# Buffer places: bias columns on the right side, pads, weights first

## The chip, the cores and the metric

The kernel runs on one core of one Trainium2 chip. The metric is the time of one execution in microseconds of the device, the median of several runs. The core has TensorE (PE; its weight loads are shown apart as PEld), VectorE (DVE), ScalarE (ACT), GpSimd (POOL) and SyncE (SP), which only issues DMAs here. They share the on-chip memory SBUF, in which an address counts the bytes along one of 128 partitions. Matmul results go to PSUM.

## The reference

One layer of a decoder trunk, x of 2048 x 1024 in float32. An RMSNorm, a projection to 4096 columns, then two branches: a diagonal complex state-space layer (S5) with a GLU, and a causal pooling mixer; both gated and merged, projected and added to x, and a last RMSNorm:

```python
h = _rmsnorm(x, norm_g[l])
proj = h @ w_in[l] + b_in[l]
ua, za, ub, zb, ga, gb = jnp.split(proj, SPLITS, axis=-1)
ya = _s5_branch(ua, ..., ssm_w_glu[l], ssm_b_glu[l])
ya = ya * jax.nn.silu(za)
yb = _pool_branch(ub, pool_w[l], pool_scale[l]) * jax.nn.silu(zb)
merged = (jax.nn.sigmoid(ga) * (ya @ w_branch_a[l])
          + jax.nn.sigmoid(gb) * (yb @ w_branch_b[l]))
x = x + merged @ w_out[l]
...
return _rmsnorm(x, final_norm_g)
```

`_s5_branch` ends in `y * sigmoid(y @ w_glu + b_glu)`.

## The kernel before, in words

Each large product is made of three matmuls in type float32r: weights and moving operand are split into a high and a low part, and `mm3` (L101 to L104) issues high x high (L102), high x low (L103) and low x high (L104). One matmul has 128x128 weights and up to 512 moving columns of 4 bytes, 2048 bytes in a partition. The 2048 positions are worked in four chunks c of 512.

The stages in order of time:
1. Norm, transposes and the first projection block (UA), into hT, the moving operand: four tiles of 32 KB a partition, high and low parts. Weights of the first two tiles lie in the rotating pool w (`wt`, two buffers), those of UA tiles 2 and 3 in `w_first2` and `w_first3` of pool d1 (L189), for all four chunks.
2. ZA projection with the scan's matrices in the background (pool d2): `matrices` (L424) loads C (`cn`) and B (`B1`, `B2`, L431, L432) by SP, and fp32 matmuls (`psk`) and transposes follow.
3. Pooling branch (UB, ZB; pool d3): the pooled tile is split into `plhl` and multiplied by `pw` into `psp`.
4. Gates GA and GB, with the scan in the background (pool d4; matmuls of 256 columns, `psx` and `psy`).
5. GLU (pools d5 and e5): weights `wg`, moving operand `yhl`, in two buffers.
6. Per chunk the branch products (weights `wt`, moving `yab`, outputs scaled by the gates `gt`), the merge into `mt`, and the output projection with `mt` as weights and `wo` as moving operand; the last piece has 256 columns. Then the final norm; its gains are the tile `gb` (L1141).

The order of the instructions is the order of the code; each engine takes its own in turn. Weights reach the matmuls through a queue of jobs: SP loads `raw` (two buffers), ScalarE makes the high part (L94), VectorE or GpSimd the low part (L96, L98), and `pump` issues one such step at fixed places.

A pool lies on the left or on the right side of SBUF. Left pools stack upwards from address 16512 (16384 bytes and four 32-byte constants lie below), right ones downwards from 229344, and a tile takes a multiple of 32 bytes. A pool that is closed gives its room to the next; an instruction that first touches such room waits for the last users of what lay there. So places set waits too. Pools in order: const, raw, w, stg (left), hT0 to hT2 (right), xp (right), par, d1 (left), and then those of the stages. const holds the bias columns `cols` and `half` (192 bytes each), `sgn` (8), `rcnt` (64), `RD` (64) and `PH` (128).

Of the kernel before, what the change touches and what calls it, by code (L numbers as in the profile page):

```python
# [9 lines left out]
F32 = mybir.dt.float32  # L10
F32R = mybir.dt.float32r
# [25 lines left out]
def hybrid_kernel(ctx: ExitStack, tc: tile.TileContext, x, norm_g, w_in, b_in, log_dt, lam_re, lam_im,  # L37
# [7 lines left out]
    outr = out[0].rearrange("(k j) d -> j k d", j=T)  # L45

    const = ctx.enter_context(tc.tile_pool(name="const", bufs=1))
    rawp = ctx.enter_context(tc.tile_pool(name="raw", bufs=2))
    wp = ctx.enter_context(tc.tile_pool(name="w", bufs=2))
    stg = ctx.enter_context(tc.tile_pool(name="stg", bufs=3))  # L50
# [4 lines left out]
    def sub(stack, name, side="left"):  # L55
        return stack.enter_context(tc.tile_pool(name=name, bufs=1, side=side, reuse_waits="tile"))
# [15 lines left out]
        return pms.tile([128, 512], F32, tag="ms", name=name)  # L72


    cols = const.tile([128, 48], F32, name="cols")
    half = const.tile([128, 48], F32, name="half")
    sgn = const.tile([128, 2], F32, name="sgn")
    rcnt = const.tile([128, 16], F32, name="rcnt")
    RD = const.tile([128, G // 2], F32, name="RD")
    PH = const.tile([128, 2, G // 2], F32, name="PH")  # L80

    def bcol(n):
        return cols[:, n:n + 1]
# [42 lines left out]
    hl = {}  # L126
# [58 lines left out]
    idn = par.tile([128, 128], F32, name="idn")  # L185
    s_d = ExitStack()
    d1 = sub(s_d, "d1")

    def w_first(key):  # L189
        t = d1.tile([128, 2, 1024], F32R, name=f"w_first{key[1]}")  # L190
        hl[key] = t
        return t[:, 0, :], t[:, 1, :], lambda r: r

    UA, ZA, UB, ZB, GA, GB = 0, 4, 8, 12, 16, 24
# [4 lines left out]
    for n in range(NB):  # L199
        w_in_job(n, plain if n < 2 else w_first)  # L200
# [10 lines left out]
    def ts(o, i, s1, o0, s2=None, o1=None):  # L211
        if s2 is None:
            V.tensor_scalar(out=o, in0=i, scalar1=s1, scalar2=None, op0=o0)
        else:
            V.tensor_scalar(out=o, in0=i, scalar1=s1, scalar2=s2, op0=o0, op1=o1)
# [6 lines left out]
    def pieces(v, bits, count):  # L222

        import struct
        if (v, bits, count) not in kept:
            res, left = [], v
            for _ in range(count - 1):
                m, e = math.frexp(left)
                q = math.ldexp(math.floor(m * 2 ** bits), e - bits)
                res.append(q)  # L230
                left -= q
            res.append(struct.unpack("f", struct.pack("f", left))[0])
            kept[v, bits, count] = res
        return kept[v, bits, count]
# [67 lines left out]
    def params(d, V, ldt, lam, dn):  # L302
# [61 lines left out]
        for h in range(2):  # L364
            r = slice(h * 64, (h + 1) * 64)
            V.tensor_copy(out=PH[r, 0], in_=ang[r, h::2])
        a0, a1, pn = PH[:, 0], PH[:, 1], d.tile([128, H], F32, name="pn")
        turn = pieces(64 * math.pi, 11, 4)
# [290 lines left out]
    def scan(d):  # L659
# [53 lines left out]
        def phases():  # L713
# [4 lines left out]
            for j in range(LV):  # L718
                ts(th[:, j], PH[:, 1], float(T << j), ALU.mult)
                ts(lo[:, j], PH[:, 0], float(T << j), ALU.mult)  # L720
            ts(n, th, 2.0 / math.pi, ALU.mult, MAGIC, ALU.add)
# [174 lines left out]
    for i in reversed(range(NB)):  # L896
# [23 lines left out]
        for k in range(2):  # L920
            n = min(T, win - 1 - k * T)
# [145 lines left out]
    for c in range(NCH):  # L1067
        t = yhl[c]
# [23 lines left out]
    d6 = sub(s_d, "d6")  # L1092
# [4 lines left out]
    def load_gate(c, n):  # L1097
        t = d6.tile([128, 2, 512], F32, tag="gt", bufs=3, name="gt")
        SP.dma_start(out=t, in_=Gd[n][c].rearrange("b p k -> p b k"))
        gts[c, n] = t  # L1100
# [22 lines left out]
    def finish(tt):  # L1123
# [12 lines left out]
            A.dma_start(out=outr[tt // 2, k0:k0 + 128, cs], in_=r[:, cs])  # L1136
        x2.pop(tt)

    load_gate(0, 0)
    load_gate(0, 1)  # L1140
    gb = d6.tile([128, D], F32, name="gb")  # L1141
# [82 lines left out]
```

## Time and profile before

| | us |
|---|---|
| median of 3 runs | 1236.32 (1235.59 to 1238.8) |
| the profiled execution | 1238.27 |
| its span, first to last instruction | 1236.4 |
| mean granted TensorE clock in it | 0.993 |

In the rows, L102 is a line of the code above, and `mm<-hT,wt` says that the instruction writes tile mm and reads hT and wt (numbers of buffers are left out). Matmuls are pipelined, so a row's duration says little of how fast they follow each other; the distance between the starts of two does. In the order of time, two neighbouring rows stand apart by that distance, to 0.01 us; over a run of many the mean is better. A bracket at a row's end is the idle time of the engine before it, and what ended it.

### The profile page before, as it was taken

What the parts mean: (1) busy time and instruction counts of PE and PEld (TensorE: products, weight loads), DVE (VectorE), ACT (ScalarE), POOL (GpSimd) and SP (SyncE); (2) the same over time, 40 slices, a digit from 0 to 9 for tenths busy, and PEclk for the clock granted to TensorE, in tenths of its full rate; (3) what the DMA queues carried; (4) which work ended last, traced back from release to release, by engine and by line L of the source; (5) the groups of instructions that cost most, each with busy time, mean ns of one, the idle gap of its engine ahead of it and who ended that gap; (6) DMA issues with size and microseconds to landing.
All of it is one profiled execution on the core that took longest, in us unless ns stands there. A gap on an engine that the chain in (4) does not pass through costs nothing. (4 is left out here: it accounts for less than half of the span.)

```text
span 1236.4 us, 14778 instructions
## 1 busy us (share of the span) xinstructions
PE 1205.5 (97%) x5413; PEld 975.1 (79%) x5413; DVE 730.8 (59%) x1310; ACT 395.3 (32%) x622; POOL 346.4 (28%) x232
## 2 busy tenths in 40 slices
PE   6999989999999999999999999999999999999996
PEld 5887867788888888888888888887878888888885
DVE  5586378153543668777788773046565855755615
ACT  6542211222222232443333432244333322322202
POOL 3321167011110212332334321234562312213312
PEclk9999989999999999999999999999999999999998
DMA  8413233201111232433334332178766553563502
GB/s 295 133 43 84 58 112 126 80 17 54 43 45 43 83 110 88 129 91 110 113 94 128 96 102 78 66 227 253 247 218 209 182 188 131 175 207 105 188 1 102
DMA packets 149783, 149.94 MB, mean 121 GB/s; under 512 B 23584, under 2 KB 111184, under 8 KB 149712
## 3 DMA queue, kind: packets, MB, share of 16 engines
q1 hardware_dynamic: 127424, 112.28, 30.6%
q10 hardware_dynamic: 22288, 36.73, 7.9%
q8 instruction: 42, 0.69, 0.2%
q14 instruction: 29, 0.24, 0.1%
HBM read 99.43 MB, written 49.55 MB: 120 GB/s over the span
## 5 line engine op out<-in xcount | busy, mean ns | idle before, releaser
L102 PE MATMUL mm<-hT,wt 128*128 128x512 f32 x960 | 382.5, 398 | 0.0
L103 PE MATMUL mm<-hT,wt 128*128 128x512 f32 x960 | 380.6, 396 | 0.0
L104 PE MATMUL mm<-hT,wt 128*128 128x512 f32 x960 | 379.9, 396 | 0.0
L104 PEld LDWEIGHTS mm<-hT,wt 128*128 128x128 f32 x960 | 180.8, 188 | 44.1
L103 PEld LDWEIGHTS mm<-hT,wt 128*128 128x128 f32 x960 | 181.1, 189 | 43.5 <-DVE hT L98 0.9
L102 PEld LDWEIGHTS mm<-hT,wt 128*128 128x128 f32 x960 | 181.2, 189 | 42.7
L96 POOL TENSOR_TENSOR wt<-raw,wt 128x1024 fp32r<-128x1024 f32 x30 | 85.5, 2849 | 316.5 <-ACT wt L94 316.5
L1027 ACT ACTIVATE go<-mm,half 128x512 f32<-128x512 f32 x64 | 43.9, 686 | 204.9 <-PE mm L104 190.2
L102 PE MATMUL mm<-yab,wt 128*128 128x512 f32 x256 | 101.2, 395 | 1.8 <-DVE gt L1160 1.8
L104 PE MATMUL mm<-yab,wt 128*128 128x512 f32 x256 | 101.0, 395 | 0.0
L103 PE MATMUL mm<-yab,wt 128*128 128x512 f32 x256 | 101.0, 395 | 0.0
L94 ACT ACTIVATE wt<-raw 128x1024 fp32r<-128x1024 f32 x62 | 65.5, 1057 | 60.7 <-PE mm L104 34.2
L1162 POOL TENSOR_TENSOR m<-gt 128x512 f32<-128x512 f32 x32 | 52.1, 1630 | 100.4 <-DVE gt L1160 71.6
L1121 POOL TENSOR_TENSOR r<-r,gb 128x512 f32<-128x512 f32 (+1 forms) x33 | 41.1, 1260 | 138.4 <-ACT xt L1118 138.3
L96 DVE TENSOR_TENSOR wt<-raw,wt 128x1024 fp32r<-128x1024 f32 x32 | 58.6, 1831 | 19.7 <-ACT wt L94 19.6
L845 ACT ACTIVATE st<-mm,half 128x512 f32<-128x512 f32 x32 | 22.1, 690 | 145.9 <-PE mm L104 114.5
L1160 DVE SCALAR_TENSOR_TENSOR gt<-gt,mm 128x512 f32<-128x512 f32 x64 | 42.3, 680 | 32.8 <-PE mm L104 27.9
L102 PEld LDWEIGHTS mm<-yab,wt 128*128 128x128 f32 x256 | 48.0, 187 | 14.4 <-issue 2.6
L104 PEld LDWEIGHTS mm<-yab,wt 128*128 128x128 f32 x256 | 48.0, 187 | 11.7
L103 PEld LDWEIGHTS mm<-yab,wt 128*128 128x128 f32 x256 | 48.0, 187 | 11.6
L104 PE MATMUL mm<-wo,mt 128*128 128x512 f32 (+1 forms) x136 | 52.0, 383 | 0.0
L103 PE MATMUL mm<-wo,mt 128*128 128x512 f32 (+1 forms) x136 | 52.0, 382 | 0.0
(272 smaller groups left out, 1920.3 us busy)
## 6 DMA issues: line engine op xcount, KB each, us to landing
xt<-in_x SPq DMA_DIRECT2D x32, 512.0 KB, 5.4
raw<-in_w_in SPq DMA_DIRECT2D x32, 512.0 KB, 4.4
Gd<-go ACTq DMA_DIRECT2D x64, 256.0 KB, 2.4
gt<-Gd SPq DMA_DIRECT2D x32, 512.0 KB, 4.8
raw<-in_w_branch_a SPq DMA_DIRECT2D x32, 256.0 KB, 3.1
raw<-in_w_branch_b SPq DMA_DIRECT2D x32, 256.0 KB, 3.5
out<-r ACTq DMA_DIRECT2D x32, 256.0 KB, 2.3
Ud<-uo ACTq DMA_DIRECT2D x16, 256.0 KB, 2.1
```

What stands on the lines that cost most here:

```text
L94: A.activation(hi, src, AF.Copy, scale=1.0 if scale is None else scale)
L96: (eng or V).tensor_tensor(out=lo, in0=src, in1=hi.bitcast(F32), op=ALU.subtract)
L102: PE.matmul(ps, lhsT=sh, rhs=mh, start=first, stop=False)
L103: PE.matmul(ps, lhsT=sh, rhs=ml, start=False, stop=False)
L104: PE.matmul(ps, lhsT=sl, rhs=mh, start=False, stop=last)
L845: A.activation(t, ps, AF.Tanh, bias=hcol(n), scale=0.5)
L1027: A.activation(o, ps, AF.Tanh, bias=hcol(n), scale=0.5)
L1121: GP.tensor_tensor(out=r, in0=r, in1=gb[:, cs], op=ALU.mult)
L1160: V.scalar_tensor_tensor(out=gt[:, b], in0=gt[:, b], scalar=1.0, in1=pss[b], op0=ALU.add, op1=ALU.mult)
L1162: GP.tensor_tensor(out=m, in0=gt[:, 0], in1=gt[:, 1], op=ALU.add)
```

## The change

It adds no instruction and moves none: on each engine the same instructions stand in the same order. It makes a second pool for constants, `constr`, on the right side, with the bias columns in it; puts an unused tile `lpad` of 192 bytes at the end of const and one of 128 bytes, `pad6`, at the start of d6; and allocates the two w_first tiles as soon as d1 is opened, ahead of its other tiles, and not when they are first used.

```diff
+    constr = ctx.enter_context(tc.tile_pool(name="constr", bufs=1, side="right"))
...
-    cols = const.tile([128, 48], F32, name="cols")
-    half = const.tile([128, 48], F32, name="half")
-    sgn = const.tile([128, 2], F32, name="sgn")
-    rcnt = const.tile([128, 16], F32, name="rcnt")
+    cols = constr.tile([128, 48], F32, name="cols")
+    half = constr.tile([128, 48], F32, name="half")
+    sgn = constr.tile([128, 2], F32, name="sgn")
+    rcnt = constr.tile([128, 16], F32, name="rcnt")
     RD = const.tile([128, G // 2], F32, name="RD")
     PH = const.tile([128, 2, G // 2], F32, name="PH")
+    const.tile([128, 48], F32, name="lpad")
...
     d1 = sub(s_d, "d1")
+    firsts = {n: d1.tile([128, 2, 1024], F32R, name=f"w_first{n}") for n in (2, 3)}
     def w_first(key):
-        t = d1.tile([128, 2, 1024], F32R, name=f"w_first{key[1]}")
-        hl[key] = t
+        t = hl[key] = firsts[key[1]]
...
+    d6.tile([128, 32], F32, name="pad6")
     load_gate(0, 0)
```

const shrinks from 672 bytes to 384, so the left pools behind it move down by 288; constr takes 480 bytes, so the right pools move down by 480. What remains of the address after the last multiple of 512 bytes, as the program allocates it:

| tile | role in matmuls | before | after |
|---|---|---|---|
| hT0 to hT3, yab, wo | moving, 512 columns (wo also 256) | 480 | 0 |
| yhl (two buffers) | moving, 512 | 288 | 0 |
| plhl | moving, 512 | 384 | 96 |
| uu, spl | moving, 256 | 288 | 0 |
| wt, wg, bt, mz, ca (scan) | weights | 288 | 0 |
| mt | weights | 160 | 0 |
| w_first2, w_first3 | weights | 192, 256 | 64, 64 |
| pw | weights | 384 | 96 |
| idn | moving in transposes | 288 | 0 |

Slices of these tiles start at multiples of 512 bytes further on (idn's one slice at its start), so they keep the remainder.

The other effect is on waits. On SP, at the start of stage 2, where the scan's matrices load (DMAHW and a number are the queues' own semaphores, PE_49 and Pool_49 those of engines), before:

```order
28 L427 DMA cn<-in_ssm_c_re 128x4x64 [waits DMAHW1_49,PE_49]
29 L427 DMA cn<-in_ssm_c_im 128x4x64 [waits DMAHW3_49]
30 L427 DMA cn<-in_ssm_c_re 128x4x64 [waits DMAHW4_49]
31 L431 DMA B_1320<-in_ssm_b_re 64x32x16 [waits DMAHW5_49]
32 L432 DMA B_1320<-in_ssm_b_im 64x32x16 [waits DMAHW6_49]
35 L478 DMA CAd_145<-ca 512x1x128 [waits DMAHW5_49,Pool_49]
```

The same place after:

```order
28 L429 DMA cn<-in_ssm_c_re 128x4x64 [waits DMAHW1_49,PE_49]
29 L429 DMA cn<-in_ssm_c_im 128x4x64 [waits DMAHW3_49]
30 L429 DMA cn<-in_ssm_c_re 128x4x64 [waits DMAHW4_49]
31 L433 DMA B_1324<-in_ssm_b_re 64x32x16 [waits DMAHW5_49,PE_49]
32 L434 DMA B_1324<-in_ssm_b_im 64x32x16 [waits DMAHW6_49]
35 L480 DMA CAd_148<-ca 512x1x128 [waits DMAHW5_49,Pool_49]
```

The first load of B1 gains a wait for a matmul: the last that reads w_first3. The first load of cn waits for the last that reads w_first2, and waited for an earlier one. On SP at the start of stage 6, before:

```order
356 L958 DMA raw<-in_w_out 128x1024 [waits DMAHW3_49,Pool_49]
357 L1099 DMA gt<-Gd_0_105 128x2x512 [waits DMAHW5_49,PE_49]
358 L1099 DMA gt<-Gd_0_109 128x2x512 [waits DMAHW0_49]
359 L1142 DMA gb<-in_final_norm_g 128x1024 [waits DMAHW1_49]
360 L1099 DMA gt<-Gd_0_113 128x2x512 [waits DMAHW2_49]
```

And after:

```order
356 L960 DMA raw<-in_w_out 128x1024 [waits DMAHW3_49,Pool_49]
357 L1101 DMA gt<-Gd_0_108 128x2x512 [waits DMAHW5_49,PE_49]
358 L1101 DMA gt<-Gd_0_112 128x2x512 [waits DMAHW0_49]
359 L1145 DMA gb<-in_final_norm_g 128x1024 [waits DMAHW1_49,PE_49]
360 L1101 DMA gt<-Gd_0_116 128x2x512 [waits DMAHW2_49]
```

The load of gb gains a wait for the last matmul that reads wg. Elsewhere VectorE's first copy into RR waits for a matmul in place of a GpSimd instruction, and the first B product into v5 for a GpSimd instruction; two ca products on GpSimd no longer wait for a DMA, one tanh of stage 2 not for GpSimd, and the first load of pwr and one of xt not for a matmul.

## Rows read from the trace of the kernel before

**Rows 1.** The page, TensorE and VectorE among the busy times

```profile
PE 1205.5 (97%) x5413; PEld 975.1 (79%) x5413; DVE 730.8 (59%) x1310; ACT 395.3 (32%) x622; POOL 346.4 (28%) x232
```

**Rows 2.** Windows by stage; stretch, length, busy us (instructions) by engine, clock, DMA

```profile
core 0: us, PE busy (x) PEld busy (x) DVE busy (x) ACT busy (x) POOL busy (x), PEclk, DMA share, GB/s
30.00:167.00 137.00, 134.08 (x628) 108.27 (x627) 85.53 (x253) 47.42 (x73) 37.74 (x20) 0.99 0.29 84
172.00:808.00 636.00, 635.08 (x2884) 514.86 (x2883) 375.14 (x618) 193.29 (x310) 159.09 (x91) 1.00 0.28 86
808.00:866.00 58.00, 56.12 (x242) 44.46 (x241) 33.58 (x38) 27.89 (x42) 21.83 (x16) 1.00 0.76 235
866.00:913.00 47.00, 45.18 (x194) 35.73 (x193) 31.63 (x27) 16.73 (x20) 26.06 (x14) 1.00 0.69 232
913.00:1221.00 308.00, 308.00 (x1328) 249.13 (x1327) 176.22 (x310) 84.68 (x135) 83.01 (x57) 1.00 0.49 155
```

**Rows 3.** Order of time, TensorE in a gate projection; start us, duration us, instruction

```profile
561.15 0.39 PE L102 MATMUL mm<-hT,wt 128*128 128x512 f32 x1
...
568.15 0.39 PE L102 MATMUL mm<-hT,wt 128*128 128x512 f32 x1
```

**Rows 4.** Order of time, TensorE, last block of stage 1, weights w_first3

```profile
118.17 0.39 PE L102 MATMUL mm<-hT,w_first 128*128 128x512 f32 x1
...
123.53 0.40 PE L104 MATMUL mm<-hT,w_first 128*128 128x512 f32 x1
```

**Rows 5.** Order of time, TensorE, output projection of the first chunk

```profile
940.52 0.40 PE L102 MATMUL mm<-wo,mt 128*128 128x512 f32 x1
...
949.85 0.40 PE L103 MATMUL mm<-wo,mt 128*128 128x512 f32 x1
```

**Rows 6.** Order of time, TensorE, GLU, chunks 0 and 1

```profile
820.79 0.39 PE L102 MATMUL mm<-yhl,wg 128*128 128x512 f32 x1
...
840.73 0.39 PE L103 MATMUL mm<-yhl,wg 128*128 128x512 f32 x1
```

**Rows 7.** Order of time, TensorE, a pooled block between two projections

```profile
303.99 0.39 PE L103 MATMUL mm<-hT,wt 128*128 128x512 f32 x1
...
304.45 0.39 PE L102 MATMUL psp<-plhl,pw 128*128 128x512 f32 x1
...
305.84 0.40 PE L102 MATMUL mm<-hT,wt 128*128 128x512 f32 x1
```

**Rows 8.** Order of time, TensorE, scan matmuls of 256 columns

```profile
459.93 0.28 PE L104 MATMUL psx<-uu,bt 128*128 128x256 f32 x1
...
460.29 0.28 PE L104 MATMUL psx<-uu,bt 128*128 128x256 f32 x1
```

**Rows 9.** The view of tile psT; count, min/median/max ns of one, first and last start

```profile
L561 PE MATMUL psT<-idn,xt x128: 270/273/476, 12.3 to 100.3; 128*128 128x128 f32 x128
```

**Rows 10.** Order of time, TensorE, sixteen transposes merged into one row

```profile
62.35 1.91 PE L561 MATMUL psT<-idn,xt 128*128 128x128 f32 x16
```

**Rows 11.** Order of time, TensorE, the two long waits before 172 us

```profile
97.52 1.73 PE L561 MATMUL psT<-idn,xt 128*128 128x128 f32 x9 [1.63 <-DVE hT L98]
...
171.69 0.66 PE L505 MATMUL psb<-idn,bp 128*128 128x128 f32 x2 [3.81 <-DVE bp L218]
```

**Rows 12.** Order of time, SP's issues of B1 and B2, first and last

```profile
120.34 0.93 SPq L431 DMA_DIRECT2D B<-in_ssm_b_re  x1
...
125.16 1.94 SPq L432 DMA_DIRECT2D B<-in_ssm_b_re  x1
```

**Rows 13.** Order of time, VectorE, the first reader of B2

```profile
149.22 0.48 DVE L215 TENSOR_SCALAR B<-B,sgn 128x512 f32<-128x512 f32 x1
```

**Rows 14.** Order of time, TensorE, the last matmul of the GLU

```profile
865.90 0.39 PE L104 MATMUL mm<-yhl,wg 128*128 128x512 f32 x1
```

**Rows 15.** Order of time, SP's issue of gb

```profile
870.50 0.92 SPq L1142 DMA_DIRECT2D gb<-in_final_norm_g  x1
```

**Rows 16.** Order of time, a weight load beside the first matmul of that block of 561 us

```profile
561.16 0.19 PEld L103 LDWEIGHTS mm<-hT,wt 128*128 128x128 f32 x1
```

## The prediction

> **What bounds the kernel now.** I read the page's busy times first, then the stages as windows, then the order of time on TensorE, where the start of one matmul is set against the start of the next. TensorE is busy for 97% of the span, VectorE for 59% [rows 1]. That share alone proves nothing, since matmuls overlap. The windows say it better: from 172 to 808 us TensorE is idle for 0.9 us of 636, from 913 to 1221 us for none of 308, at a granted clock of 1.00 [rows 2]. In both stretches nobody makes TensorE wait, so the time is the number of matmuls times the distance from one start to the next. [...]
>
> The distance differs between blocks that do the same thing:
> - projection (moving operand hT at 480 beyond a multiple of 512 bytes, weights wt at 288): 30 matmuls from 561.15 to 568.15, 233.3 ns each [rows 3];
> - the same hT with w_first3 as weights (256): 23 from 118.17 to 123.53, 233.0 ns [rows 4];
> - output projection (wo at 480, weights mt at 160): 40 from 940.52 to 949.85, 233.3 ns [rows 5];
> - GLU (yhl at 288, weights wg at 288): 88 from 820.79 to 840.73, 226.6 ns [rows 6];
> - pooled (plhl at 384, weights pw at 384): eight distances from 303.99 to 305.84, three of them pooled ones, make 1.85 us, 17 ns less than 8 x 233.3; so about 228 ns each [rows 7].
>
> With weights at 288, 256 and 160 the distance stays at 233.3 while the moving operand lies at 480; it falls where the moving operand lies elsewhere. So I take the place of the moving operand for the cause of the 6.7 ns between 233.3 and 226.7. It isn't the region: those 88 run over both buffers of yhl, the second of which lies among the addresses that hT3 had. No row has a moving operand of 512 columns at 0.
>
> A check that the distances are all there is: 913 to 1221 us holds 1,320 matmuls of 512 columns; times 233.3 ns that is 308.0 us, the whole stretch [rows 2, 5].
>
> **The change part by part.** Order and number of instructions stay; what changes is addresses, and the waits that follow from who now lies where.
>
> *Addresses.* 4,584 matmuls of 512 columns have their moving operand moved from 480 to 0: 3,072 on hT, 768 on yab, 744 on wo. The cost of one at 0 is not in the trace. [...] From above: 0 could be one step worse than 480, 240 ns, as 480 is one step worse than 288. I take 226.7, the nearest row: GLU is the only long run whose two operands lie at the same place modulo 512, as they all will.
>
> [...]
>
> By stage, at 6.67 ns for each:
> - 172 to 808 us: 2,472 matmuls, 16.5 us; 913 to 1221 us: 1,320, 8.8 us. Both have no slack to lose it in [rows 2].
> - 30 to 167 us: 505 matmuls, 3.4 us. At its ends TensorE waits for VectorE, 1.63 us before 97.52 and 3.81 us before 171.69 [rows 11]. Those chains don't start from TensorE alone, so some of the gain becomes a longer wait: I keep half, 1.7 us.
> - 808 to 866 us: 48 projections, 0.3 us; the GLU gains nothing by this value.
> - 866 to 913 us: 192 on yab would give 1.3 us, but there TensorE is already idle for 1.8 us of 47 with the DMA engines at 0.69 [rows 2]; weights come from memory and set the pace. I count nothing.
> - First 30 us and the tail after 1221 us: nothing; the 48 matmuls of 256 columns in the tail are worth at most 0.3 us.
>
> Sum 27.3 us. The 48 pooled matmuls go from 384 to 96 and not to 0 (d3's tiles behind ub are not padded), and the 192 with w_first weights get their weights at 64. I count nothing for either: 48 x 6.67 = 0.3 us at most, and the weights' place made no difference [rows 3 to 5].
>
> *Waits.* Putting w_first first in d1 lays them under the tiles that stage 2 loads at its start. SP's load of B1 then waits for the last matmul on w_first3, which starts at 123.53 [rows 4]; before it went out at 120.34 [rows 12]. Queued behind it are three more loads of B1 and B2, the last of which ended its issue at 125.16 + 1.94 = 127.1; now some 3.5 us later, 130.6. VectorE needs them at 149.22 [rows 13], 18.6 us later. Without that cover it would cost 3.5 us. VectorE's first copy to RR now waits for the same matmul, but stands behind zo, which needs the block after it; nothing. The load of gb now overlaps wg by 128 bytes and waits for the last GLU matmul, begun at 865.90 [rows 14]; SP came to it at 870.50 only [rows 15], so nothing. Where a wait goes (tanh of the first silu on GpSimd, a ca product on a DMA, pwr and one xt load on a matmul) the others that remain came later; nothing. Other engines' operands move too; the same VectorE and ScalarE forms run in tiles at several offsets with like durations, and neither bounds a long stretch, so nothing.
>
> The profiled execution took 1238.27 us around a span of 1236.4; the median of three is 1236.32, 1.95 less. 1238.27 - 27.3 = 1211.0, and against the median **1209.0 us**.
>
> **The rivals.**
> [...]
> 2. *No change.* The 6.7 ns belong to the GLU for another reason than the address (its weights' halves lie 8 KB apart, wt's 4 KB), or 0 counts as 480 does. For: 480 is only 32 bytes short of the next multiple. Against: the pooled block has neither trait and is quicker than 233.3 too. 1236 us.
> 3. *Slower.* Each weight load starts with the matmul before it, 561.16 beside 561.15 [rows 16], so two streams read SBUF at once. Today they start 192 to 320 bytes apart modulo 512 in the 4,584; after the change both at 0. If equal places collide, each costs a step more, 240 ns: 25.3 us in the free stretches and 3.7 us elsewhere, 1265 us. It decides as soon as the projection's distance is above 233.3. Against: the GLU and the pooled block start both operands at equal places and are the quickest.
>
> **How the numbers follow.** Chances: forecast with its smaller mishaps 0.49, rival 1 in any size 0.20, rival 2 0.17, rival 3 0.14. A difference of 0.3%, 3.7 us, is about what can be told from none. So faster 0.69, same 0.17, slower 0.14. The forecast's own range is 1201 to 1218: the step at 6 to 8 ns, and the early stages' gain kept whole or lost. The range for 8 in 10 takes in no change (1239 with the runs' spread) and reaches to half of rival 1, at 1172; it leaves out rival 3 and the far end of rival 1, about 0.2.
>
> **What would show it.** [...] The GLU must stay at 226.6. The stretch that is now 913 to 1221 us must take 299 us. The waits before 97.52 and 171.69 may grow by up to a microsecond each. B1 must land before VectorE asks for it. I am wrong if the distances fall and the time doesn't, which would mean that loads or VectorE pace the long stretches after all.

## The result: 1216.2 us after 1236.3, ratio 0.983

The changed kernel has a median of 1216.20 us (1215.82 to 1216.58, four runs); the kernel before, beside it, 1236.33. The ratio is 0.9834 [0.9817, 0.9851]. A second set of runs gave 1217.85 beside 1236.48, ratio 0.9850 [0.9833, 0.9867]. The forecast of 1209.0 had the direction, and the size of the step in the distance from start to start; it gave the step a cause that x1 and x2 below refute, and was 7.2 us too far. The profiled execution took 1216.58 us around a span of 1214.7; the span before was 1236.4.

The page, TensorE and VectorE among the busy times, to be set against [rows 1]:

```profile
PE 1180.5 (97%) x5413; PEld 976.0 (80%) x5413; DVE 731.5 (60%) x1310; ACT 395.0 (33%) x622; POOL 345.9 (28%) x232
```

TensorE is still busy for 97%, as before: the share says nothing of a gain of 22 us. The distance from start to start says it. The order of time on TensorE, the same matmuls as in [rows 3 to 6] (gate projection, w_first3, GLU, output projection); columns are start us, duration us, instruction:

```profile
550.88 0.39 PE L104 MATMUL mm<-hT,wt 128*128 128x512 f32 x1
...
557.68 0.39 PE L104 MATMUL mm<-hT,wt 128*128 128x512 f32 x1
...
117.30 0.40 PE L104 MATMUL mm<-hT,w_first 128*128 128x512 f32 x1
...
122.67 0.39 PE L106 MATMUL mm<-hT,w_first 128*128 128x512 f32 x1
...
805.87 0.39 PE L104 MATMUL mm<-yhl,wg 128*128 128x512 f32 x1
...
825.81 0.39 PE L105 MATMUL mm<-yhl,wg 128*128 128x512 f32 x1
...
925.43 0.39 PE L104 MATMUL mm<-wo,mt 128*128 128x512 f32 x1
...
934.50 0.39 PE L105 MATMUL mm<-wo,mt 128*128 128x512 f32 x1
```

Over 30 distances the projection now makes 226.7 ns (before 233.3), the GLU 226.6 over 88 (unchanged), the output projection 226.8 over 40 (before 233.3). The block on w_first3 makes 5.37/23 = 233.5: **no gain**, though its moving operand lies at 0 like the others'. Its weights lie at 64.

Both traces hold the same 5,413 matmuls in the same order, so the start of one and the same matmul can be compared. Stage by stage, named by the times of the kernel before:

| stage before, us | length before | after | gain | forecast |
|---|---|---|---|---|
| 30.2 to 171.7 | 141.49 | 140.48 | 1.0 | 1.7 |
| 172.1 to 215.2 | 43.05 | 41.54 | 1.5 | 0.9 |
| 215.2 to 430.0 | 214.86 | 209.91 | 4.9 | 5.8 |
| 430.0 to 808.2 | 378.16 | 371.51 | 6.6 | 9.8 |
| 808.2 to 866.1 (last gate projections, GLU) | 57.92 | 61.38 | -3.5 | 0.3 |
| 866.1 to 913.2 (first branch products) | 47.09 | 43.91 | 3.2 | 0 |
| 913.2 to 1220.4 | 307.15 | 299.45 | 7.7 | 8.8 |

(The forecast's 16.5 us for 172 to 808 is divided here by its 137, 867 and 1,468 matmuls on hT.) The same as windows of the changed kernel, from the second row on with the stretches of 172 to 808 joined, as in [rows 2]; columns are stretch, length, busy us (instructions) by engine, granted clock, DMA share, GB/s:

```profile
170.67:793.63 622.96, 619.13 (x2884) 515.04 (x2883) 374.93 (x618) 193.25 (x310) 158.95 (x91) 1.00 0.28 88
793.63:855.01 61.38, 57.80 (x242) 45.52 (x240) 35.50 (x39) 29.36 (x44) 24.15 (x17) 0.97 0.73 231
855.01:898.91 43.90, 43.76 (x193) 35.98 (x192) 30.79 (x27) 14.96 (x17) 23.58 (x13) 1.00 0.72 239
898.91:1198.37 299.46, 299.46 (x1322) 247.78 (x1321) 175.12 (x305) 84.60 (x135) 82.72 (x57) 1.00 0.50 159
```

TensorE, which was idle for 0.9 us in the long stretch, is now idle for 3.8 (622.96 - 619.13). The view of waits on TensorE says for whom; columns are waiter, releaser, us in total, times, longest:

```profile
PE psy L105 <- DVE spl L98: 3.1, 3, 1.0
PE mm L104 <- ACT yhl L96: 3.0, 2, 2.6
```

And in the order of time, the first of the three waits for spl, then the one in the GLU:

```profile
522.79 0.28 PE L104 MATMUL psy<-spl,ca 128*128 128x256 f32 x1
524.09 0.39 PE L105 MATMUL psy<-spl,ca 128*128 128x256 f32 x1 [1.03 <-DVE spl L98]
...
838.45 0.39 PE L106 MATMUL mm<-yhl,wg 128*128 128x512 f32 x1
841.47 0.49 PE L104 MATMUL mm<-yhl,wg 128*128 128x512 f32 x1 [2.63 <-ACT yhl L96]
```

The three distances at spl are 1.30, 1.30 and 1.31 us; the same three were 0.41, 0.41 and 0.42 before, here the first of them:

```profile
533.36 0.28 PE L102 MATMUL psy<-spl,ca 128*128 128x256 f32 x1
533.77 0.39 PE L103 MATMUL psy<-spl,ca 128*128 128x256 f32 x1
```

So 2.7 us of the gain turned into waits for VectorE. The distance in the GLU is 3.0 us (2.0 before), and 1 us behind it the clock falls:

```profile
837.00:841.00 4.00, 1.84 (x9) 1.19 (x7) 2.20 (x3) 1.27 (x2) 1.36 (x1) 1.00 0.74 249
842.62:846.03 3.41, 3.31 (x8) 2.03 (x7) 2.56 (x4) 2.92 (x5) 0.00 (x0) 0.50 1.06 338
```

For 3.4 us the granted clock is 0.50, after a wait in which TensorE stood idle for 2.6 us; six matmuls start there where fifteen would have. The kernel before has no such half-speed record there, and neither has the second profile of the changed kernel, whose two long distances there are 0.9 and 1.9 us: it lost 1.9 us from 808 to 866 us, not 3.5, and gained 1.6 from 866 to 913, not 3.2. So these two rows of the table differ between executions of one kernel; their sum, -0.3, is the same in both.

### The profile page after: what moved, and what is told of

Read it like the earlier page. It is cut to its first block, busy times and chain, and to the rows that moved or that the text cites. A ratio compares the mean times of both kernels' runs of the same rounds, so it can differ in the third digit from the quotient of the medians.

```text
span 1214.7 us, 14777 instructions
## 1 busy us (share of the span) xinstructions
PE 1180.5 (97%) x5413; PEld 976.0 (80%) x5413; DVE 731.5 (60%) x1310; ACT 395.0 (33%) x622; POOL 345.9 (28%) x232
## 5 line engine op out<-in xcount | busy, mean ns | idle before, releaser
L104 PE MATMUL mm<-hT,wt 128*128 128x512 f32 x960 | 377.2, 393 | 0.0
L105 PE MATMUL mm<-hT,wt 128*128 128x512 f32 x960 | 375.6, 391 | 0.2 <-DVE hT L100 0.2
L106 PE MATMUL mm<-hT,wt 128*128 128x512 f32 x960 | 374.9, 390 | 0.0
L104 PE MATMUL mm<-yab,wt 128*128 128x512 f32 x256 | 99.9, 390 | 0.1
L105 PE MATMUL mm<-yab,wt 128*128 128x512 f32 x256 | 99.7, 389 | 0.0
L106 PE MATMUL mm<-yab,wt 128*128 128x512 f32 x256 | 99.7, 389 | 0.0
```

The source lines that it names most:

```text
L104: PE.matmul(ps, lhsT=sh, rhs=mh, start=first, stop=False)
L105: PE.matmul(ps, lhsT=sh, rhs=ml, start=False, stop=False)
L106: PE.matmul(ps, lhsT=sl, rhs=mh, start=False, stop=last)
```

## The experiments

Three theories of the distance. **M**, the prediction's: the place of the moving operand decides. **R**: the difference between the places of moving operand and weights decides, and equal places are quick. **A**: both have to lie at a multiple of 512 (or 128). Places are given as moving/weights, modulo 512.

**x1, equal places that are no multiple.** The kernel before with two pads only:

```diff
     PH = const.tile([128, 2, G // 2], F32, name="PH")
+    const.tile([128, 48], F32, name="lpad")
...
+    d6.tile([128, 32], F32, name="pad6")
     load_gate(0, 0)
```

> The kernel before with two pads only (192 bytes at the end of const, 128 at the start of d6): moving operand and weights lie at the same remainder, 480, in projections, branch products and output projection; nothing lies at a multiple of 512; GLU 480/480, w_first2 at 384 and w_first3 at 448 against hT at 480. Theory R (what counts is the difference between the places of the moving operand and of the weights loaded beside it; zero is quick): 226.7 ns a matmul as in the changed kernel, 233.3 in the w_first blocks, 1214 to 1219 us. Theory M, the prediction's (the place of the moving operand counts, 480 is a bad one): 233.3 ns everywhere, the GLU too, so about 1237 us. Theory A (both operands have to lie at a multiple of 512, or of 128): 233.3 ns everywhere, the GLU too, about 1237 us.

Measured: 1219.11 us (1216.97 to 1220.98), ratio 0.9851 [0.9833, 0.9868], span 1215.1. The same block of the projection, now 480/480, then the w_first3 block, 480/448:

```profile
551.39 0.39 PE L103 MATMUL mm<-hT,wt 128*128 128x512 f32 x1
...
558.20 0.39 PE L103 MATMUL mm<-hT,wt 128*128 128x512 f32 x1
...
117.79 0.40 PE L103 MATMUL mm<-hT,w_first 128*128 128x512 f32 x1
...
123.16 0.40 PE L105 MATMUL mm<-hT,w_first 128*128 128x512 f32 x1
```

6.81/30 = 227.0 ns with hT where it always was; 233.5 where the weights lie 32 bytes off. M and A fall: neither the move of hT to 0 nor the multiple of 512 is needed. From 215 to 808 us this kernel is as quick as the changed one (581.40 and 581.42 us): the pads of x1 give the whole gain there, and the bias columns on the right side and the w_first tiles put first add nothing to it.

**x2, the moving operand at 0 and the weights elsewhere.** The changed kernel without one line:

```diff
-    const.tile([128, 48], F32, name="lpad")
```

> The changed kernel without the 192-byte tile lpad: right pools stay at a remainder of 0 (hT, yab, wo), left pools go to 320 (wt, wg, yhl, mt, scan). Theory M (place of the moving operand): hT, yab and wo still at 0, so 226.7 ns and 1215 to 1218 us. Theory R (difference of the two): 320 apart in projections, branch products and output projection, so 233.3 ns there and about 1236 us; GLU 320/320 stays at 226.7. Theory A (both at a multiple): about 1237 us, GLU at 233.3.

Measured: 1239.70 us, ratio 1.0017 [1.0007, 1.0026]: the whole gain is gone. Projection (0/320) and GLU (320/320):

```profile
559.82 0.39 PE L103 MATMUL mm<-hT,wt 128*128 128x512 f32 x1
...
566.82 0.39 PE L103 MATMUL mm<-hT,wt 128*128 128x512 f32 x1
...
819.50 0.39 PE L103 MATMUL mm<-yhl,wg 128*128 128x512 f32 x1
...
839.45 0.39 PE L104 MATMUL mm<-yhl,wg 128*128 128x512 f32 x1
```

233.3 ns and 226.7 ns. This is the sharpest of the runs: hT, yab and wo lie where the change put them, and nothing is gained.

**x3, the last blocks brought into line.** The changed kernel with

```diff
+    d1.tile([128, 112], F32, name="pad1")
     firsts = {n: d1.tile([128, 2, 1024], F32R, name=f"w_first{n}") for n in (2, 3)}
...
+    d3.tile([128, 104], F32, name="pad3")
```

> The changed kernel plus a pad of 448 bytes ahead of the w_first tiles and one of 416 in d3: w_first2, w_first3, pw and plhl now at a remainder of 0 too. Theory R: 192 matmuls on w_first go from 233.4 to 226.7 ns, 1.3 us, of which the wait at the end of stage 1 may take a part; 48 pooled ones keep their equal places and their distance; 1214.9 to 1215.8 us. Theory M: no change, 1216.2 us. Theory A: w_first and pooled, 1.3 + 0.3 us, 1214.6 us.

Measured: 1215.02 us, ratio 0.9825 [0.9807, 0.9842], span 1211.6. The intervals of the two medians overlap, so it is read in the trace, last block on w_first3:

```profile
115.91 0.39 PE L104 MATMUL mm<-hT,w_first 128*128 128x512 f32 x1
...
121.13 0.39 PE L106 MATMUL mm<-hT,w_first 128*128 128x512 f32 x1
```

5.22/23 = 227.0 ns, as R has it. From 30 to 124 us (by the times of before) the kernel takes 91.9 us, the changed one 93.6 in its first profile, with a half-speed record behind the wait for hT (granted clock 0.50 for 3.4 us), and 92.7 in its second, without one as here: so 0.8 of the 1.3 us at stake arrive. From 215 to 430 us it falls by another 0.8, which R's expectation of "keep their distance" missed: that is the 48 pooled matmuls. Their own two places were equal in the changed kernel too (96/96), but they come in threes between projections at 0/0, and the eight distances of [rows 7] made 1.86 us there and make 1.81 here, 226 ns each. So equal places of its own were not enough for the block: at 96/96 between projections at 0/0, it and the matmuls behind it go slower than at 0/0. From the first matmul of that block to the twelfth behind it, in the changed kernel and then here:

```profile
299.23 0.40 PE L104 MATMUL psp<-plhl,pw 128*128 128x512 f32 x1
...
302.01 0.39 PE L104 MATMUL mm<-hT,wt 128*128 128x512 f32 x1
...
297.31 0.39 PE L104 MATMUL psp<-plhl,pw 128*128 128x512 f32 x1
...
300.03 0.39 PE L104 MATMUL mm<-hT,wt 128*128 128x512 f32 x1
```

The twelve distances make 2.78 us, 232 ns each, where the projections further on are at 227 again, and 2.72 here.

**x4, other differences** in the whole kernel: pads of 64 bytes in const, 480 ahead of wg, 256 ahead of the odd yhl, 384 in d6, and w_first at 496 and 4.

> A map of differences (moving minus weights, modulo 512), hT, yab, wo at 0: projections and branch products 128 (wt at 384), output projection 384 (mt at 128), w_first2 16 (weights at 496), w_first3 508 (weights at 4), GLU chunks 0 and 2 at 32 (384 against 352), chunks 1 and 3 at 256 (96 against 352), scan 0 (384/384). Theory R with a period of 512: 226.7 ns nowhere among the 512-column matmuls, 233.3 in all of them, about 1238 us. With a period of 256: the odd GLU chunks alone at 226.7. With a period of 128: projections, branch products, output projection and odd GLU chunks at 226.7, about 1217 us. What 16 and 4 bytes apart give is open: 226.7 if only whole 32-byte steps count. Theory M: everything on hT, yab, wo at 226.7, whatever the weights; about 1217 us.

Measured: 1237.85 us (one run). Means over all distances within the blocks: projection and branch 0/384, 232.6 and 232.4 ns; output projection 0/128, 232.4; GLU 384/352, 233.3; GLU 96/352, 227.7 with a median of 227; w_first 0/496, 227.0 to 228.3; 0/4, 232.3. M falls again; 256 apart is quick and 128 is not, which speaks for a period of 256.

**m1, a map.** A kernel that leaves the layer out and has a row of matmuls by itself, 30 for each case:

```python
for j in range(30):
    m0, w0 = 1024 * (j % 2) + a // 4, 1024 * (j % 2) + b // 4
    PE.matmul(t[:, 0:n], lhsT=wt[:, w0:w0 + 128], rhs=mv[:, m0:m0 + n], start=j == 0, stop=j == 29)
```

> A kernel that leaves the whole computation out: one long row of float32r matmuls, 30 for each case, weights and moving operand alternating between two places 4096 bytes apart, and nothing that makes TensorE wait. Cases: 512 columns with the moving operand at 0 and the weights 0 to 508 bytes further on; both at the same place p, p from 4 to 480; weights at 0 and the moving operand 4 to 496 further on; then 256 and 384 columns. Theory R (only the difference counts): 226.7 ns for a difference of 0 at every common place p that is a multiple of 32; 233.3 for 32, 64, 96, 192, 224, 320, 448; 226.7 for 256 again, if its period is 256 as the odd GLU chunks at 96/352 suggest; the same with the signs turned. Theory M: 226.7 in all rows with the moving operand at 0. Theory A: 226.7 only with both at multiples of 128. Open: differences under 32 bytes (16 gave 227 to 228, 4 gave 232.3), and 256 columns, where equal places seem the slower (120 against 113.6 ns at 320 apart).

In the order of time each case is one merged row, its 30 matmuls from the first start to the last end; less the last one's 0.39 us, a 29th of it is the distance. Cases 0/0, 0/32, 0/256, 4/4, 480/480:

```profile
37.87 6.97 PE L75 MATMUL maa<-mv,wt 128*128 128x512 f32 x30
93.45 7.15 PE L75 MATMUL mai<-mv,wt 128*128 128x512 f32 x30
176.90 6.99 PE L75 MATMUL mau<-mv,wt 128*128 128x512 f32 x30
266.91 7.29 PE L75 MATMUL mbh<-mv,wt 128*128 128x512 f32 x30
321.96 7.01 PE L75 MATMUL mbp<-mv,wt 128*128 128x512 f32 x30
```

From the starts, 512 columns, moving operand at 0, ns:

| weights further on by | 0 | 4 | 16 | 32 | 64 | 128 | 192 | 240 | 248 | 252 |
|---|---|---|---|---|---|---|---|---|---|---|
| distance | 226.7 | 232.4 | 233.3 | 233.1 | 233.2 | 232.3 | 229.2 | 227.3 | 233.3 | 226.7 |
| 256 more | 227.4 | 232.4 | 233.3 | 233.4 | 233.4 | 232.3 | 229.0 | 227.3 | 233.3 | 226.7 |

The two rows agree within 0.7 ns, as much as two takes of 0/0 differ (226.7 and 227.4): with the moving operand at 0 the period of 256 is shown. R holds for places at multiples of 32 (32/32 227.3, 64/64 227.6, 256/256 226.8, 480/480 228.1), but not as a law for any place: 16/16 gives 231.2 and 4/4 237.6, the worst of all, and 16/0 gives 231.4 where 0/240, the same difference modulo 256, gives 227.3. Fine differences have a pattern of their own.

Then where the rest of the gain went, all from x3.

**x5, a fourth sza buffer** for the GLU (`bufs=3` to `bufs=4`). SP loads sza, the gate's tiles, and yraw, the GLU's input; its output yao goes through one of three stg buffers to YAd in memory.

> The kernel x3 (all operands at 0) with four sza buffers in place of three. Theory S (the GLU lost 3.7 us because SP, held for a free sza buffer, issues the yraw load of chunk 3 some 10 us after its buffer is free): the four sza loads issue at once, yraw leaves about 8 us earlier, the wait of 3.3 us at the start of GLU chunk 3 and the half-speed record behind it go, and 808 to 913 us (by the places of before) falls from 104.6 to about 99 us; 1207 to 1211 us. Theory D (the DMA engines set the pace of the whole stretch from 808 to 913 us, 0.73 busy): the wait comes back on the weights of the branch products, and the stretch stays at 104 to 105 us; 1214 to 1216 us.

Measured: 1213.56 us, one run. The four sza loads do go out at once, but yraw leaves at 834.20 us (x3: 834.10). ScalarE, VectorE, SP and TensorE around it:

```profile
831.95 0.69 ACT L1085 ACTIVATE yao<-mm,half 128x512 f32<-128x512 f32 x1 [4.88 <-DMA YAd<-yao]
...
832.73 1.44 DVE L1087 SCALAR_TENSOR_TENSOR yao<-yao,yraw 128x512 f32<-128x512 f32 x1 [4.83 <-ACT yao L1085]
...
834.20 2.07 SPq L1008 DMA_DIRECT2D yraw<-Yd  x4
...
838.81 0.76 PE L104 MATMUL mm<-yhl,wg 128*128 128x512 f32 x1 [2.45 <-ACT yhl L96]
```

Theory S falls as it was put. The yraw buffer comes free with the last yao product at 832.73 + 1.44 = 834.17, and that waits on ScalarE, which waits 4.9 us for a stg buffer to be written out to YAd. From 808 to 913 us x5 takes 102.9 us (x3: 104.6), between the two expectations; the half-speed record of the GLU is 3.4 us long in it and 6.8 in x3, so the difference can't be put down to the edit.

**x8, both holds taken away**: the fourth yao in a buffer of its own, and the fourth sza load behind yraw:

```diff
+        if c:
+            gate_y(c, NB - 1)
...
-                gate_y(c + 1)
-            o = stg.tile([128, 512], F32, tag="stg", name="yao")
+                gate_y(c + 1, 0, NB - 1)
+            o = (d5 if i == NB - 1 else stg).tile([128, 512], F32, tag="last" if i == NB - 1 else "stg", name="yao")
```

> The kernel x3 with two changes around the GLU: the fourth yao of each chunk gets a buffer of its own (the three stg buffers are held until their YAd write has landed, which held the last reader of yraw back in x5), and the fourth sza load with its product moves behind the yraw load of the next chunk. Theory S2 (the wait at chunk 3 comes from the release of the yraw buffer, through yao, stg and YAd): yraw of chunk 3 leaves SP at about 827 us and not at 834, the wait of 3.3 us before chunk 3 and the half-speed record behind it go, the GLU's last two chunks take 22 to 24 us instead of 28.2, and 808 to 913 us (by the places of before) 99 to 101 us instead of 104.6; about 1209 us. Theory D (the transfers pace the stretch as a whole): TensorE waits for weights of the branch products or the output projection instead, and the stretch stays at 104 to 105 us.

Measured: 1213.09 us, one run. yraw leaves at 829.73, the long wait and the half-speed record are gone, and the last two GLU chunks take 23.1 us (x3: 28.2). But the branch products give most of it back; windows of the GLU with the last gate projections, and of the first branch products, and the view of waits:

```profile
792.03:848.00 55.97, 55.44 (x241) 44.71 (x240) 35.88 (x40) 29.47 (x44) 21.43 (x15) 1.00 0.80 254
848.00:894.66 46.66, 44.37 (x193) 35.81 (x192) 31.74 (x25) 15.08 (x17) 26.49 (x14) 1.00 0.67 222
```

```profile
PE mm L104 <- DVE gt L1167: 2.3, 2, 1.4
```

5.1 us less in the first and 3.1 more in the second: 102.6 us for both (x3: 104.6). In the kernel before the two made 105.0, in the changed one 105.3. So against x3 three fifths of the gain in the GLU turn into waits for the gate products, waits that the kernel before has too (two, 1.8 us). How much of the 2.0 us left is the edit's is not shown: the same stretch of x9 below, which leaves this code as x3 has it, took 105.1 us in one profile, with a half-speed record in the GLU, and 103.2 in another without one. Neither theory is decided.

**x6, spl's low part on GpSimd** in place of VectorE (`V` to `GP` in its split).

> The kernel x3 with the low part of spl made by GpSimd and not by VectorE, where it stands behind the table of the next unit. Theory V (the scan's three long waits of 1.3 us are TensorE arriving earlier at a product that VectorE delivers no earlier than before): the second psy matmul on spl follows the first without a long wait in all units (waits at 520, 596 and 671 us gone), 430 to 808 us falls by 2.5 to 3 us from 371.5 and 215 to 430 us by up to 1 us. Rival (the waits belong to the slot: ACT's high part comes late as well, or GpSimd takes over 3 us): the waits stay above 1 us.

Measured: 1213.87 us, one run; 430 to 808 us is 371.46, unchanged: the fall of 2.5 to 3 us did not come. The waits at spl are gone and stand a dozen matmuls later, at bt, which VectorE makes. GpSimd, VectorE and TensorE, in the order of time:

```profile
518.33 2.65 POOL L98 TENSOR_TENSOR spl<-sp,spl 128x1024 fp32r<-128x1024 f32 x1 [3.06 <-ACT spl L96]
...
518.76 2.37 DVE L742 TENSOR_TENSOR tab<-tmp 128x128 f32<-128x128 f32 x1
...
524.12 0.38 PE L106 MATMUL psx<-uu,bt 128*128 128x256 f32 x1 [1.01 <-DVE bt L98]
```

The table step of 2.37 us takes 0.29 in x9: beside the GpSimd subtraction VectorE's step took 2.1 us longer, and ended 0.15 us behind it. Another VectorE row, a pair of table steps from 513.00 us on, took 2.39 us beside a GpSimd subtraction that ran from 512.88 to 515.27, and takes 0.26 in x9; what held it is not shown. So x6 put one wait in the place of another, and does not decide between V and its rival.

**x9, the table behind the splits** in VectorE's order:

```diff
-            if u + 1 < NU:
-                table(u + 1)
             yield
             run_taps(u)
...
                 cut(bt, bhl, V)
+                table(u + 1)
```

> The kernel x3 with the scan's table of the next unit moved behind the splits of spl and bt in VectorE's order. Theory V: VectorE's table is what delivers spl (and in x6 bt) too late; with it behind, the waits of 1.3 us at 520, 596 and 671 us go, and 215 to 808 us falls by 2.5 to 4 us from 580.6; about 1211 us. Rival: the table then delays gelu and the next run_scan, and the wait comes back as a wait for psx readers, spl of the next unit or a PSUM buffer, so that 215 to 808 us stays at 580 us or grows.

Measured: 1209.49 us in one run, and in four more:

> x9 timed in rounds: its one profiled span of 1207.7 us had a first stage (up to 30 us) 1.6 us shorter than the kernel before, which the edit can't give; without that 1209.3 plus 2 us around the span: 1210 to 1212 us, ratio 0.979 to 0.981.

1210.23 us, ratio 0.9788 [0.9771, 0.9806]. 430 to 808 us takes 367.65, 3.9 less than x3, and no distance there is above 0.32 us. The two matmuls at the first of the three waits:

```profile
522.39 0.28 PE L104 MATMUL psy<-spl,ca 128*128 128x256 f32 x1
522.50 0.28 PE L105 MATMUL psy<-spl,ca 128*128 128x256 f32 x1
```

Their distance is 0.11 us. Against the kernel before, the stretch is 10.5 us shorter: the forecast's 9.8 and the 1.2 that the three waits had cost there already (0.4 each), less 0.5 by a smaller step (below). Theory V holds: VectorE's order took the missing 2.7 us.

**x10, x8 and x9 together, and the changed kernel beside it.**

> x8 and x9 together. x9 took 3.9 us out of 430 to 808 us, x8 took 2.0 us net out of 808 to 913 us and gave 0.7 back behind it. If the two add up: 1.3 us below x9, 4 to 7 us below the changed kernel: 1209 to 1212 us, ratio to before 0.978 to 0.981. If the stretch behind 808 us is paced by its transfers, which start earlier with the rest, it is no better than x9.

> The changed kernel once more, beside the two: 1215 to 1218 us, ratio 0.983 to 0.985.

x10: 1210.16 us (1208.60 to 1210.81), ratio 0.9788 [0.9773, 0.9804], no better than x9. Its stretch from 808 to 913 us takes 102.0 us, 1.1 less than x9's in the same set of runs, and from 913 on it loses 1.8 against x9, one profile each. The changed kernel gave 1217.85. So x9, with the pads of x3, is the quickest kernel that the runs support, 0.6% below the changed one.

## Why the prediction was right, and where it failed

*The distance.* 233.3 to 226.7 ns was the term that carried the sum, and it came as forecast on hT, yab and wo. The rivals are out. Rival 1 is a second step below 226.7: no run shows the term for it, nor the 1172 us that the range takes from it, and no block of 512 columns read in the runs goes below 226.6 ns a distance. Rival 2 needs 233.3. Equal places at multiples of 32 don't collide with 512 columns (rival 3; 226.7 to 228.1 ns in m1); at 4/4 (237.6 ns), and with 256 columns (119.8 at 0/0, 113.4 at 0/64), they are the slower ones (m1). One row that was held against the rivals was misread, though. In the pooled block of the kernel before, the next row is

```profile
305.15 0.39 PE L102 MATMUL mm<-hT,wt 128*128 128x512 f32 x1
```

and from 304.45 [rows 7] that is 0.70 us for the three pooled distances, 233 ns each and not 228. The 17 ns were saved in the distances around them, and the GLU alone spoke for equal places.

*The step that failed* is "I take the place of the moving operand for the cause", with "the weights' place made no difference". x1 and x2 show the contrary twice over. The rows of before could not tell: every long slow block had unequal places, and the one long quick one, the GLU, equal places, 288/288. The sentence that "GLU is the only long run whose two operands lie at the same place modulo 512" held the answer and was used to choose a value, not a cause. The size came out right because the change makes places equal wherever it moves hT, yab and wo, but for w_first. To that extent the number was luck: by the cause as stated, x2 had to gain as much, and it gained nothing.

*What that cost.* The 192 matmuls at 0/64 gained nothing: 192 x 6.67 = 1.3 us. Of the 505 matmuls of the early stages 313 were left, worth 2.1 us, of which half was to be kept; 1.0 us came. But the two waits that were to take the other half did not grow: they are 1.57 and 3.9 us, after 1.63 and 3.81, and the second profile, without the half-speed record behind the first of them, gains 1.9. The pooled blocks, counted at nothing, lost 0.8 us.

*172 to 808 us*: 16.5 forecast, 13.1 measured. The mis-sized term is "no slack to lose it in": 2.7 us went to the three waits for spl and 0.8 to the pooled blocks. The kernel before already waited there, 0.41 us at 533.4, 609.6 and 685.8, inside its 0.9 idle us of 636 [rows 2]: such small waits show which engine is next. A half-speed record after the wait for bp (granted clock 0.50), shorter by luck of this execution (3.4 us for 6.8; 6.8 again in the second profile, where 172 to 808 us gains 12.1), gave 0.6 back; the last 0.5 is that the distance between projections from 430 to 808 us fell by 6.4 ns on the mean (233.4 to 227.0) and not by 6.67.

*808 to 913 us*: 0.3 forecast, -0.3 measured, as a sum of -3.5 and +3.2 (-1.9 and +1.6 in the second profile). "The GLU gains nothing" was right for its distance and said nothing of its waits; "I count nothing" for the branch products was wrong alone and right for the pair.

*913 to 1221 us*: 8.8 forecast, 7.7 measured. Before, the mean over the stage was 307.15/1,320 = 232.7 and not the 233.3 of the 40 that were read, and after it is 226.9.

*The waits of the edits.* B1 waits as foreseen, and nobody for it; SP's issue after, and VectorE's first reader, to be set against [rows 12] and [rows 13]:

```profile
123.09 0.74 SPq L433 DMA_DIRECT2D B<-in_ssm_b_re  x1
...
127.19 1.56 SPq L434 DMA_DIRECT2D B<-in_ssm_b_re  x1
...
147.78 0.48 DVE L217 TENSOR_SCALAR B<-B,sgn 128x512 f32<-128x512 f32 x1
```

The last of the four loads is out at 128.75, 19 us before VectorE comes to B. gb is issued at 857.17, 2 us behind the last GLU matmul.

*The sum.* 27.3 us were forecast and the span fell by 21.7. The misses: 3.4 in 172 to 808, 1.1 in 913 to 1221, 0.7 in the early stages, 0.6 in 808 to 913; the first 30 us gave 0.5, the tail took 0.3. The other 1.6 of the 7.2 us are the step from the profiled execution to the median: 1.95 us before, 0.4 after.

## What to carry to other kernels

Read the distance from start to start of matmuls that wait for nothing, block by block, beside both operands' addresses: here two unused tiles of 192 and 128 bytes took 1.5% off a kernel that keeps TensorE busy for 97% of its time (x1). For float32r matmuls of 512 columns with a weight load each, as here, make weights and moving operand equal modulo 256 with both at multiples of 32 (226.7 to 228.1 ns in m1, 227.7 at 96/352 in x4, against 233.1 to 233.4 for weights 32 or 64 bytes further on), in the long runs and in the short blocks between them; no absolute place was needed (227.0 at 480/480 in x1). When the bounding engine gets quicker, look for the smallest waits that it already had: here they grew from 0.4 to 1.3 us, and reordering the engine behind them (VectorE's table) gave 3.9 us.

## What the runs showed that was not expected

- Two reads of TensorE alone, weights and moving operand, change its pace by their places: 226.7 to 237.6 ns for the same 512 columns, at a mean granted clock of 0.981 over the execution, with no other engine at work but ScalarE, which copies each finished case out once (m1). Which part of the memory makes the difference is not shown, nor whether the weights that count are a matmul's own or those that load beside it for the next: in every long block the two lie alike.
- With 256 columns equal places are not the quickest. m1 at 0/0 and 0/64, 119.8 and 113.4 ns:

```profile
377.53 3.75 PE L75 MATMUL mbx<-mv,wt 128*128 128x256 f32 x30
388.22 3.57 PE L75 MATMUL mca<-mv,wt 128*128 128x256 f32 x30
```

- The last piece of the output projection, 47 distances of 256 columns, shows it in the kernel: 5.54 us before (480/160), 5.63 after (0/0), 5.34 in x2 (0/320).
- The stretch from TensorE's first matmul to the one that starts at 30.2 us before took between 21.1 and 24.7 us in the profiled executions, whatever the edit; differences of 1 us between spans can't be put down to an edit without the stages.
